# Second layer of a two-layer trunk step: the order of raw weight loads, of the attention's last splits, and of one split in the feed-forward slots

## The chip, the cores and the metric

The kernel runs on one core of one Trainium2 chip. A core has TensorE (PE, matmuls), VectorE (DVE), ScalarE (ACT), GpSimd (POOL) and SyncE (SP); each works through its own instructions in order, and they wait for each other by semaphores. SP here only issues transfers (DMA) between the chip's memory (HBM) and the on-chip memory; its queue is in order too, so a transfer that waits for its buffer holds back all that stand behind it. Matmul results go to PSUM. The metric is the device time of one execution in microseconds; the figure for the kernel is the median of three runs.

## The reference

The trunk has two layers over 128 prompt tokens and 512 sample tokens. Layer 0 mixes tokens by latent attention and pooling, layer 1 by neighbourhood attention (8 heads) and windowed attention (8 heads). Both end in a convolutional feed-forward network. The change lies in layer 1 alone:

```python
for l in range(DEPTH):
    hp = modulate(rmsnorm(xp, norm_mix[l]), mp[:, 0], mp[:, 1])
    hs = modulate(rmsnorm(xs, norm_mix[l]), ms[:, 0], ms[:, 1])
    ...
        op, kv_na, kv_sw = odd_context(hp, w_in_odd[e], swa_sink[e], w_out_odd[e])
        os_ = odd_latent(hs, cache_na_kv[:, e], cache_swa_kv[:, e], w_in_odd[e], na_rpb[e],
                         swa_sink[e], w_out_odd[e])
    ...
    xp = xp + mp[:, 2] * op
    xs = xs + ms[:, 2] * os_
    hp = modulate(rmsnorm(xp, norm_ffn[l]), mp[:, 3], mp[:, 4])
    hs = modulate(rmsnorm(xs, norm_ffn[l]), ms[:, 3], ms[:, 4])
    xp = xp + mp[:, 5] * conv_ffn(hp, w_up[l], conv_w[l], conv_b[l], w_down[l])
    xs = xs + ms[:, 5] * conv_ffn(hs, w_up[l], conv_w[l], conv_b[l], w_down[l])
```

The last matmul of both attentions is `concat(o_na, o_sw) @ w_out`, 1024 by 1024; `conv_ffn` is `(silu(g) * a) @ w_down` with `a` and `g` from a three-tap convolution of `h @ w_up`.

## The kernel before

Activations lie transposed: 8 tiles of 128 features by 642 columns (512 sample tokens, a gap, 128 prompt tokens). They are worked in two halves of columns, `EVEN`, 322 and 320 wide. The first half's parts are called `ha`, the second's `hb`.

**Products in three.** Every float32 operand is split into a high and a low part in the matmul's own format: ACT casts the high part (`split`, line 117), then another engine subtracts it from the source to get the low part (`low`, line 113, on DVE or POOL). A product then takes three matmuls for each pair of tiles: high by high, high by low, low by high. A first half of the output projection for one tile of 128 outputs is 8 x 3 = 24 matmuls of 322 columns.

**End of the attention.** `odd` works through 16 heads, two at a time in each other's shadow; the order of the steps is written out by hand as strings. `ODD_END` (line 84) is the string for the last head: `t` turns probabilities (PE transposes into `tr`, ACT copies to `pt`), `l` is the low part of `pt` on DVE, `w` weighs values (PE, into `o`), `o` and `po` add up outputs, `fo` fetches a raw tile of `w_out` for the two early products, `fs` splits it (tiles `whi`, `wlo`), and `pa` splits the attention output of one more finished pair of heads (`put_act`, line 730, into the tuples `oT`). There are 8 pairs; six `pa` steps stand in the string, and the rest is split behind it, first half and then second half.

**Early products.** `run` computes the first half of output tiles 0 and 1 (`early`) while the pool of the weights, `weights`, is still open; it reads `oT[0]` in the order 4, 5, 6, 7, 0, 1, 2, 3, which is the order in which the pairs were finished.

**Output projection.** Then `weights` is closed, a new pool `ffn1` (`pm`) opens in the same memory, and `begin` (line 1665) runs. A pool lays its tiles out in the order in which their names first appear. In `begin` these were `ht` (the sums for the feed-forward products), `x` (the residual stream), `raw` (loaded weights, three buffers). A tile's first writer waits for whatever lay there and is still in use. The first half runs over j = 0..7 (0 and 1 are the early ones): `parts(j, engine)` splits the raw weight of tile j into `w`, `add_x` adds the product to `x` on DVE (line 1605), `square` squares it on ACT. The second half runs over 3, 4, 5, 6, 7, 1, 2, 0.

**Feed-forward.** `w_up` times the normed activations is done by a scheme with 7 block products in place of 8: blocks A11, A12, A22, S1 to S4 are sums of weight blocks, p1 to p7 the products, U2 and U3 sums of products that DVE adds up (`plus`, line 1965). `slot` (line 2028) is one of the 22 tiles of the hidden width from f = 4 on, 18 of them: while PE does p1, p6, p7, p5, p2, p4, p3 of tile f, POOL makes the sums for tile f + 1 (lines 1901 to 1906), ACT and DVE or POOL split its blocks, and DVE does the additions. p3 adds into the bank of p5, so it comes after the addition (`c22`) that reads p5's result. Between p3 and the next p1 come products with `w_down`. The first slot also convolves tile 3 (`conv`).

The order on each engine is the order of the code (`manual_schedule`).

Of the kernel before, what the change touches and what calls it, by code (L numbers as in the profile page):

```python
# [81 lines left out]
jf pe m.3 e.3 n.0.a l.3 l.4 je.d w.2 pn r.2 w.3 w.4 n.1.d n.2.d r.3 n.3.d je.d o  # L82
"""]
ODD_END = """
fo.0 fo.1 t.0 pt l.0 pa t.1 fs.0 pa pl pw pa l.1 po w.0 t.2 fs.1 pa w.1 t.3 l.2 t.4 pa l.3 je w.2 w.3 pa l.4 w.4 o
"""
JOBS = ("q", 5), ("v", 1), ("q", 6), ("v", 2), ("q", 7), ("k", 0), ("q", 0), ("k", 1), ("q", 1), ("k", 2), ("q", 2), ("k", 3), ("q", 3), ("v", 3)

# [1 line left out]
class Trunk:  # L90
# [873 lines left out]
    def odd(self, pool, h, oT, bias_full, psums):  # L964
# [389 lines left out]
        def issue(plan, at, u, v):  # L1354
            nonlocal bias_next, put
            for step in plan.split():
                name, *arg = step.split(".")
                engine = arg.pop() if arg and arg[-1].isalpha() else "p"
                eng = nc.vector if engine == "d" else nc.gpsimd
                n = int(arg[0]) if arg else 0  # L1360
                if name == "j":
                    for _ in range(n):
                        job_step(at)
                elif name == "jf":
                    while job_step(at):
                        pass
                elif name == "jr":
                    job_weights(eng)
                elif name == "je":
                    job_part(at, eng)  # L1370
                elif name == "br" and at < 15:
                    bias_next = bias_of(at - 7)
                elif name == "bs" and at < 15:
                    bias_sum(*bias_next)
                elif name == "pa" and not jobs and job is None and put < (at - 1) // 2:
                    self.put_act(oT, (put + 4) % 8, o32[put], eng, EVEN)
                    put += 1
                elif name == "s" and u:
                    scores(u, n)
                elif name == "m" and u:  # L1380
                    maxima(u, n)
                elif name == "e" and u:
                    exps(u, n)
                elif name == "r" and u:
                    over(u.s, slice(n, n + 1))
                elif name == "n" and u:
                    normed(u, n, engine)
                elif name == "t" and v:
                    turn(v, n)
                elif name == "l" and v:  # L1390
                    v.t[n][3]()
                elif name == "w" and v:
                    weigh(v, n)
                elif name == "o" and v:
                    outputs(v)
                elif name == "sp" and u:
                    prompt_scores(u)
                elif name == "sv" and u:
                    prompt_take(u)
                elif name == "pe" and u and u.last:  # L1400
                    prompt_exps(u)
                elif name == "pn" and u and u.last:
                    prompt_normed(u)
                elif name == "pt" and v and v.last:
                    prompt_turn(v)
                elif name == "pl" and v and v.last:
                    v.pt[2]()
                elif name == "pw" and v and v.last:
                    prompt_weigh(v)
                elif name == "fo":  # L1410
                    self.w_first.append(self.fetch(i["w_out"][1, n], D))
                elif name == "fs":
                    self.w_first[n] = self.w_first[n](nc.gpsimd)
                elif name == "po" and v and v.last:
                    prompt_outputs(v)

        o32, v, bias_next, put, self.w_first = [], None, None, 0, []
        with self.psums(psums[1]), self.tc.manual_schedule(engines=ENGINES):
            job_load()
            with self.pool("odd_masks") as pa:  # L1420
# [20 lines left out]
                    v = u  # L1441
                issue(ODD_END, 16, None, v)
                for half in range(2):
                    for n in range(put, 8):
                        self.put_act(oT, (n + 4) % 8, o32[n], halves=EVEN, only=(half,))


# [94 lines left out]
class Mix:  # L1542
# [122 lines left out]
    def begin(self, po, oT, xsrc, early):  # L1665
# [4 lines left out]
        def load_x(j):  # L1670
            self.x[j] = self.T(self.pm, "x", [P, 2 * HB], F32, 8)
            nc.sync.dma_start(self.x[j][:, 0:W], xsrc[:, j, :])
            G.memset(self.x[j][:, W : 2 * HB], 0.0)

        def load(j, with_x=True):
            raw[j] = self.T(self.pm, "raw", [P, D], F32, 3)
            nc.sync.dma_start(raw[j], t.i["w_out"][l, j])
            if with_x:
                load_x(j)
# [6 lines left out]
        def product(j, half):  # L1686
            return self.out_product(w[j], oT, half)

        first = [self.pair(po, "first", 4) for _ in n_]
        second = [self.pair(po, "second", 4) for _ in n_]  # L1690
        rr = [self.T(po, "rs", [P, HB], F32, 3) for _ in range(3)]
        tile = lambda: self.T(po, "sq", [P, HB], F32, 3)
        ht = [[self.T(self.pm, "ht", [P, 3, HB], F32R, 8) for _ in range(2)] for _ in n_]
        load_x(0), load_x(1)
        for j in range(2, 5):
            load(j)
        parts(2, V), load(5), parts(3, G), load(6)
        sqs, sqs1 = [], []
        for j in range(KT):
# [328 lines left out]
    def slot(self, f, pv, nx, downs):  # L2028
# [11 lines left out]
        def sums(part):  # L2040
            if nx is not None:
                self.sums(nx, part)
# [7 lines left out]
        self.copy1(f)  # L2050
        conv("silu")
        self.p6(f)
        self.u2(f), sums(1), conv("aid"), block("S2")
        self.p7(f)
        self.u3(f), conv("tapa", "mul"), block("S3")
        for d in downs[:1]:
            self.parts_d(*d)
        for d in downs[2:3]:
# [267 lines left out]
```

## Time and profile before

| | |
|---|---|
| median of 3 runs (1704.79 to 1714.16) | 1706.52 us |
| profiled execution | 1716.46 us, its span 1714.7 us |
| mean granted clock of PE | 0.971 |
| busy in the span: PE, DVE, ACT, POOL | 1588.6, 1266.2, 929.1, 776.2 us |
| attention of layer 1 ends, early products begin | 1170.09 us |
| first product behind the early ones begins | 1188.42 us |
| first slot's wait of PE | 6.49 us, to 1324.83 |

In a row of the timeline stand the start, the length of a run of equal instructions, engine, line, operation, tiles, shape and count; in brackets how long the engine had been idle before it and what ended that. In a row of stretches stand the busy time of each engine with its instructions, the clock granted to PE (1.00 is full), the share of DMA in use and GB/s. In a row of groups stand the count, busy us, the mean ns of one and the engine's idle time before them. Matmuls overlap, so a run's length is a little more than the distance to the next.

### The profile page before, as it was taken

What the parts mean: (1) busy time and instruction counts of PE and PEld (TensorE: products, weight loads), DVE (VectorE), ACT (ScalarE), POOL (GpSimd) and SP (SyncE); (2) the same over time, 40 slices, a digit from 0 to 9 for tenths busy, and PEclk for the clock granted to TensorE, in tenths of its full rate; (3) what the DMA queues carried; (4) which work ended last, traced back from release to release, by engine and by line L of the source; (5) the groups of instructions that cost most, each with busy time, mean ns of one, the idle gap of its engine ahead of it and who ended that gap; (6) DMA issues with size and microseconds to landing.
All of it is one profiled execution on the core that took longest, in us unless ns stands there. A gap on an engine that the chain in (4) does not pass through costs nothing.

```text
span 1714.7 us, 28130 instructions
## 1 busy us (share of the span) xinstructions
PE 1588.6 (93%) x10349; PEld 1514.9 (88%) x10349; DVE 1266.2 (74%) x2183; ACT 929.1 (54%) x1792; POOL 776.2 (45%) x711
## 2 busy tenths in 40 slices
PE   8877888888999999999998999987997999999996
PEld 2777777788999999999997999986997999999996
DVE  4886788768899778977638777774687667777766
ACT  3554767645655335533445677874465344444435
POOL 2154677554234333433063244655235455555443
PEclk9998999989999999999999999998999999999999
DMA  9431212053344444544235211114222223222221
GB/s 339 136 105 49 62 51 80 13 174 124 117 148 145 153 139 143 155 152 136 68 107 169 59 50 53 50 39 138 86 84 75 78 73 98 82 77 73 78 73 63
DMA packets 79032, 175.62 MB, mean 102 GB/s; under 512 B 11598, under 2 KB 29342, under 8 KB 78894
## 3 DMA queue, kind: packets, MB, share of 16 engines
q1 hardware_dynamic: 76398, 169.55, 30.8%
q10 hardware_dynamic: 2304, 4.20, 0.7%
q8 instruction: 82, 1.34, 0.3%
q14 instruction: 56, 0.46, 0.1%
q0 software_dynamic: 192, 0.07, 0.0%
HBM read 166.71 MB, written 8.03 MB: 102 GB/s over the span
## 4 chain that ended last, share of the span: by engine, by line
PE 54%; DVE 12%; issue 6%; ACT 4%; POOL 3%; DMA 3%; SPq 0%; DVEq 0%; POOLq 0%; ACTq 0%
PE mm L137 26%; PE p L1594 22%; DMA mraw<-in_w_mod_dram 2%; DVE acc L316 1%; PE sc L1209 1%; DVE wlo L113 1%; PE tr L1247 1%; PE o L1259 1%; DVE nt L424 1%; DMA raw<-in_w_out_dram 1%; POOL w L113 1%; DVE ha L438 1%; ACT whi L117 1%; PE sc L137 0%; PE o L851 0%
## 5 line engine op out<-in xcount | busy, mean ns | idle before, releaser
L314 POOL TENSOR_TENSOR acc<-acc,mt 128x512 f32<-128x512 f32 x115 | 175.9, 1530 | 266.3 <-ACT mt L313 251.5
L137 PE MATMUL mm<-ha,whi 128*128 128x352 f32 (+1 forms) x1168 | 288.7, 329 | 4.7 <-ACT ha L437 4.6
L137 PE MATMUL mm<-hb,whi 128*128 128x290 f32 (+1 forms) x1168 | 244.9, 303 | 1.1 <-ACT hb L437 1.1
L137 PEld LDWEIGHTS mm<-ha,whi 128*128 128x128 f32 (+1 forms) x1168 | 203.3, 191 | 6.6 <-ACT ha L437 4.7
L316 DVE SCALAR_TENSOR_TENSOR acc<-mraw,cs,acc 128x512 f32<-128x512 f32 (+1 forms) x165 | 170.5, 1040 | 48.0 <-DMA mraw<-in_w_mod_dram 46.4
L137 PEld LDWEIGHTS mm<-hb,whi 128*128 128x128 f32 (+1 forms) x1168 | 193.6, 192 | 3.9 <-issue 2.7
L137 PE MATMUL mm<-ha,wlo 128*128 128x352 f32 (+1 forms) x584 | 189.5, 325 | 0.0
L113 POOL TENSOR_TENSOR wlo<-raw,whi 128x1024 fp32r<-128x1024 f32 (+3 forms) x47 | 100.5, 2143 | 175.1 <-ACT whi L117 107.2
L137 PE MATMUL mm<-hb,wlo 128*128 128x290 f32 (+1 forms) x584 | 175.2, 300 | 0.0
L113 POOL TENSOR_TENSOR w<-raw,w 128x512 fp32r<-128x512 f32 (+1 forms) x68 | 89.5, 1327 | 177.0 <-ACT w L117 177.0
L137 PE MATMUL mm<-g,whi 128*128 128x352 f32 (+1 forms) x704 | 157.5, 311 | 6.5 <-DVE x L447 5.2
L117 ACT CAST whi<-raw 128x1024 fp32r<-128x1024 f32 (+3 forms) x117 | 115.9, 995 | 69.0 <-PE mm L137 52.7
L313 ACT ACTIVATE mt<-mraw,cs 128x512 f32<-128x512 f32 x115 | 81.8, 721 | 111.7 <-DMA mraw<-in_w_mod_dram 99.4
L1594 PE MATMUL p<-g,d 128*128 128x320 f32 (+1 forms) x912 | 140.4, 312 | 1.0 <-POOL d L113 0.9
L1594 PEld LDWEIGHTS p<-g,d 128*128 128x128 f32 x912 | 136.9, 190 | 2.5 <-POOL d L113 2.1
L1594 PE MATMUL p<-hb,w 128*128 128x322 f32 (+1 forms) x816 | 129.5, 313 | 7.8 <-DVE cg L1965 6.5
L1594 PEld LDWEIGHTS p<-hb,w 128*128 128x128 f32 x816 | 123.5, 191 | 9.0 <-DVE cg L1965 6.8
L1594 PE MATMUL p<-ha,w 128*128 128x322 f32 x768 | 123.0, 315 | 5.8 <-ACT w L117 4.0
L137 PEld LDWEIGHTS mm<-g,whi 128*128 128x128 f32 x704 | 118.3, 189 | 8.6 <-ACT ha L437 3.8
L1594 PEld LDWEIGHTS p<-ha,w 128*128 128x128 f32 x768 | 117.5, 192 | 6.8 <-ACT w L117 4.3
L137 PEld LDWEIGHTS mm<-hb,wlo 128*128 128x128 f32 (+1 forms) x584 | 112.8, 193 | 0.0
L137 PEld LDWEIGHTS mm<-ha,wlo 128*128 128x128 f32 (+1 forms) x584 | 110.4, 189 | 0.5
(332 smaller groups left out, 3773.7 us busy)
## 6 DMA issues: line engine op xcount, KB each, us to landing
raw<-in_w_up_dram SPq DMA_DIRECT2D x90, 512.0 KB, 3.6
mraw<-in_w_mod_dram SPq DMA_DIRECT2D x128, 256.0 KB, 2.9
raw<-in_w_out_dram SPq DMA_DIRECT2D x19, 512.0 KB, 4.2
raw<-in_w_in_odd_dram SPq DMA_DIRECT2D x18, 512.0 KB, 3.5
mraw<-in_w_mod_dram SPq DMA_DIRECT2D x16, 512.0 KB, 8.8
raw<-in_w_down_dram SPq DMA_DIRECT2D x16, 512.0 KB, 3.6
draw<-in_w_down_dram SPq DMA_DIRECT2D x40, 192.0 KB, 2.4
raw<-in_w_down_dram SPq DMA_DIRECT2D x16, 384.0 KB, 3.1
```

The lines of the kernel that those rows point to most:

```text
L113: (engine or self.nc.vector).tensor_sub(lo, src, Fv(hi))
L117: self.nc.scalar.copy(hi, src)
L137: self.pe = self.nc.tensor.matmul(out, lhsT=l, rhs=r, start=k == 0, stop=k == n - 1)
L313: nc.scalar.activation(t, raw, AF.Copy, scale=s)
L314: nc.gpsimd.tensor_add(acc, acc, t)
L316: nc.vector.scalar_tensor_tensor(out=acc, in0=raw, scalar=s, in1=acc, op0=ALU.mult, op1=ALU.add)
L424: self.nc.vector.scalar_tensor_tensor(out=t[:, c], in0=x[k][:, c0:c1][:, c], scalar=self.mod[l][:, ma, k, v : v + 1], in1=rs[:, c], op0=AL ...
L438: nc.vector.scalar_tensor_tensor(out=lo[:, c], in0=t[:, c], scalar=ss, in1=Fv(hi[:, c]), op0=ALU.add, op1=ALU.subtract)
L1209: nc.tensor.matmul(ps[:, c : c + n], lhsT=u.Q[:, a], rhs=x[e], start=e == 0, stop=e == 1)
L1247: nc.tensor.transpose(tp[:, j * P : (j + 1) * P], u.p[b][:, x : x + P], self.ident)
L1259: nc.tensor.matmul(u.o[:, u.t[c][2]], lhsT=v, rhs=u.t[c][e], start=c == 0 and e == 0, stop=c == 4 and e == 1)
L1594: self.t.pe = self.nc.tensor.matmul(ps[:, 0:n], lhsT=l_, rhs=r[:, 0:n], start=first and m == 0, stop=last and m == count - 1, skip_group_c ...
```

## The change

Four edits in the code of layer 1. In `ODD_END` the second early weight's low part goes to DVE (`fs.1.d`), and `fs` takes the engine from the string. `pa` splits the first half of an attention output alone; the second halves of all eight follow behind the first halves of the last two. In `begin` the raw tiles of output tiles 2, 3 and 4 are made and loaded first, ahead of `ht` and of `x`, so that `raw` lies at the start of the pool. In `slot` the split of block S2 of tile f + 1 stands behind the addition for U3.

```diff
-fo.0 fo.1 t.0 pt l.0 pa t.1 fs.0 pa pl pw pa l.1 po w.0 t.2 fs.1 pa w.1 t.3 l.2 t.4 pa l.3 je w.2 w.3 pa l.4 w.4 o
+fo.0 fo.1 t.0 pt l.0 pa t.1 fs.0 pa pl pw pa l.1 po w.0 t.2 fs.1.d pa w.1 t.3 l.2 t.4 pa l.3 je w.2 w.3 pa l.4 w.4 o
...
-                    self.put_act(oT, (put + 4) % 8, o32[put], eng, EVEN)
+                    self.put_act(oT, (put + 4) % 8, o32[put], eng, EVEN, (0,))
...
-                    self.w_first[n] = self.w_first[n](nc.gpsimd)
+                    self.w_first[n] = self.w_first[n](eng)
...
-                    for n in range(put, 8):
+                    for n in range(0 if half else put, 8):
...
+        for j in range(2, 5):
+            load(j, False)
         first = [self.pair(po, "first", 4) for _ in n_]
...
-        load_x(0), load_x(1)
-        for j in range(2, 5):
-            load(j)
+        for j in range(5):
+            load_x(j)
...
-        self.u2(f), sums(1), conv("aid"), block("S2")
+        self.u2(f), sums(1), conv("aid")
         self.p7(f)
-        self.u3(f), conv("tapa", "mul"), block("S3")
+        self.u3(f), block("S2"), conv("tapa", "mul"), block("S3")
```

On SP, where the output projection's loads begin, before; `x` tiles are the residual stream, `raw` tiles the weights, and in brackets stand the semaphores that a load waits for:

```order
L1024 DMA out_na_v_dram<-kvo_12901 128x128 [waits DMAHW5_49,Activation_49]
L1672 DMA x_13241<-x_mid 128x642 [waits PE_49,Pool_49]
L1672 DMA x_13244<-x_mid 128x642
L1677 DMA raw_13247<-in_w_out_dram 128x1024 [waits DMAHW0_49]
L1672 DMA x_13249<-x_mid 128x642 [waits DMAHW1_49]
L1677 DMA raw_13252<-in_w_out_dram 128x1024 [waits DMAHW2_49]
L1672 DMA x_13254<-x_mid 128x642 [waits DMAHW3_49]
```

The same place now:

```order
L1024 DMA out_na_v_dram<-kvo_12901 128x128 [waits DMAHW5_49,Activation_49]
L1677 DMA raw_13222<-in_w_out_dram 128x1024 [waits DMAHW4_49,DVE_49]
L1677 DMA raw_13224<-in_w_out_dram 128x1024 [waits DMAHW0_49,Pool_49]
L1677 DMA raw_13226<-in_w_out_dram 128x1024 [waits DMAHW3_49,Pool_49]
L1672 DMA x_13247<-x_mid 128x642 [waits DMAHW1_49,PE_49]
L1672 DMA x_13250<-x_mid 128x642 [waits DMAHW2_49,PE_49]
L1672 DMA x_13253<-x_mid 128x642
```

The first load waited for a matmul of the first early product (the last that reads `wlo`, over which `x` lay) and for POOL; now it is a weight and waits for DVE, whose instruction is the low part of the second early weight (`wlo_13074` below). The first `x` waits for PE transposes and scores of the last heads.

On DVE, at the end of the attention, before (`o_2407` is the last pair's output, `ha` and `hb` are halves of attention outputs, `w` is the weight of output tile 2):

```order
L1329 TENSOR_TENSOR o_2407_12759<-tr_13057,ot_13071 64x128
L113 TENSOR_TENSOR pt_13083<-tr_13078,pt_13082 128x384 [waits Activation_49]
L113 TENSOR_TENSOR pt_13104<-tr_13099,pt_13103 128x384 [waits DVE_49,Activation_49]
L113 TENSOR_TENSOR pt_13111<-tr_13107,pt_13110 128x256 [waits Activation_49]
L1267 TENSOR_TENSOR o_2407_12759<-o_13075,ot_13137 64x4x8x16 [waits Activation_49]
L113 TENSOR_TENSOR ha_13141<-o_2326_12390,ha_13140 128x322 [waits Activation_49]
L113 TENSOR_TENSOR ha_13145<-o_2407_12759,ha_13144 128x322 [waits Activation_49]
L113 TENSOR_TENSOR hb_13149<-o_2326_12390,hb_13148 128x320 [waits Activation_49]
L113 TENSOR_TENSOR hb_13153<-o_2407_12759,hb_13152 128x320 [waits Activation_49]
```

The same place now, up to the third of the eight second halves:

```order
L1329 TENSOR_TENSOR o_2407_12759<-tr_13049,ot_13059 64x128
L113 TENSOR_TENSOR wlo_13074<-raw_13013,whi_13073 128x1024 [waits DMAHW4_49,Activation_49]
L113 TENSOR_TENSOR pt_13071<-tr_13066,pt_13070 128x384 [waits DVE_49,PE_49]
L113 TENSOR_TENSOR pt_13088<-tr_13083,pt_13087 128x384 [waits DVE_49,Activation_49]
L113 TENSOR_TENSOR pt_13095<-tr_13091,pt_13094 128x256 [waits Activation_49]
L1267 TENSOR_TENSOR o_2407_12759<-o_13063,ot_13113 64x4x8x16 [waits Activation_49]
L113 TENSOR_TENSOR ha_13117<-o_2326_12390,ha_13116 128x322 [waits Activation_49]
L113 TENSOR_TENSOR ha_13121<-o_2407_12759,ha_13120 128x322 [waits Activation_49]
L113 TENSOR_TENSOR hb_13125<-o_1850_10200,hb_13124 128x320 [waits Activation_49]
L113 TENSOR_TENSOR hb_13129<-o_1911_10508,hb_13128 128x320 [waits Activation_49]
L113 TENSOR_TENSOR hb_13133<-o_1993_10886,hb_13132 128x320 [waits Activation_49]
```

The low part of the second early weight has come from POOL to DVE and stands ahead of three `pt` low parts; six `hb` low parts have come from POOL to DVE and stand ahead of the first `w`.

On DVE, in the first slot (f = 4), one piece of the difference; `ca_14603` is U2's sum, the `cg` with it is U3's, `w` from `s` is S2's low part:

```order
-L1965 TENSOR_TENSOR ca_14603<-p_14606,ca_14603 128x322
-L113 TENSOR_TENSOR w_2805_14626<-s_14594,w_2804_14625 128x512
-L1965 TENSOR_TENSOR cg_14642<-p_14629,ca_14603 128x322
-L1996 SCALAR_TENSOR_TENSOR v_14623<-ca_14513,convw,v_14623 128x641 x2
-L2019 TENSOR_TENSOR va_14646<-v_14623,cg_14514 128x642
+L1997 SCALAR_TENSOR_TENSOR v_14565<-cg_14514,convw,v_14565 128x641 x2
+L1966 TENSOR_TENSOR ca_14603<-p_14606,ca_14603 128x322
+L1966 TENSOR_TENSOR cg_14638<-p_14625,ca_14603 128x322
+L113 TENSOR_TENSOR w_2807_14641<-s_14594,w_2806_14640 128x512
+L1997 SCALAR_TENSOR_TENSOR v_14623<-ca_14513,convw,v_14623 128x641 x2
+L2020 TENSOR_TENSOR va_14646<-v_14623,cg_14514 128x642
```

The addition for U3 has changed places with S2's low part.

## Prediction

> **What bounds the kernel now.** I read the busy time by stretches first, then the timeline of TensorE (PE) where it is not full, then what the others did there. All times are us from the span's start.
>
> ```profile
> 1180.00:1200.00 20.00, 15.71 (x86) 15.18 (x85) 6.15 (x11) 7.05 (x14) 5.13 (x6) 0.85 0.88 292
> 1200.00:1220.00 20.00, 20.00 (x135) 19.84 (x134) 7.56 (x18) 5.33 (x10) 2.53 (x2) 1.00 0.23 77
> 1400.00:1500.00 100.00, 99.82 (x671) 99.08 (x670) 74.82 (x128) 44.02 (x78) 55.23 (x44) 1.00 0.26 81
> ```
>
> The columns are PE, its weight loads, DVE, ACT, POOL, clock, DMA share and GB/s. Behind 1200 PE is the bound: 135 matmuls in 20 us is 148 ns each, and in the slots (1400 to 1500) only 0.18 us of 100 is idle. In 1180 to 1200 it is neither full nor at full clock. This is the seam between the attention of layer 2 and its output projection:
>
> ```profile
> 1170.09 0.74 PE L1594 MATMUL p<-ha,whi 128*128 128x322 f32 x2
> ...
> 1173.16 0.41 PE L1594 MATMUL p<-ha,whi 128*128 128x322 f32 x1 [0.47 <-POOL ha L113]
> ...
> 1175.19 0.41 PE L1594 MATMUL p<-ha,whi 128*128 128x322 f32 x1 [1.33 <-POOL ha L113]
> ...
> 1176.97 0.64 PE L1594 MATMUL p<-ha,whi 128*128 128x322 f32 x1 [0.95 <-POOL ha L113]
> ...
> 1188.42 0.57 PE L1594 MATMUL p<-ha,w 128*128 128x322 f32 x2 [3.99 <-ACT w L117]
> 1189.28 23.03 PE L1594 MATMUL p<-ha,w 128*128 128x322 f32 x142 [0.30 <-DVE w L113]
> ```
>
> From 1170.09 on PE runs the two early products (2 x 24 matmuls), then the six other first halves (6 x 24, the 2 + 142 of the last rows), to 1189.28 + 23.03 = 1212.31. That is **42.2 us for 192 matmuls**, where 192 x 148 ns is 28.4. Of the 13.8 too many, 0.47 + 1.33 + 0.95 + 3.99 + 0.30 = **7.0 are waits**: three for POOL's low halves of `ha`, two for the first raw weights. The other **6.8 are half clock**:
>
> ```profile
> 1170.00:1172.00 2.00, 2.00 (x10) 0.50 0.00 0
> ...
> 1178.00:1180.00 2.00, 2.00 (x9) 0.50 0.04 8
> 1180.00:1182.00 2.00, 2.00 (x10) 0.50 0.49 138
> ...
> 1186.00:1188.00 2.00, 0.00 (x0) 1.00 0.98 360
> ...
> 1190.00:1192.00 2.00, 2.00 (x9) 0.50 1.01 317
> ...
> 1194.00:1196.00 2.00, 2.00 (x16) 1.00 0.83 323
> ```
>
> The clock column falls to 0.50 some us after a gap (1190 to 1192, behind the 3.99 us), and then 9 or 10 matmuls fit where 15 or 16 do later. The weights are late because of one queue:
>
> ```profile
> SPq L1672 <- PE p L1594: 26.4, 1, 26.4
> ...
> 1181.02 0.42 SPq L1677 DMA_DIRECT2D raw<-in_w_out_dram  x1
> ...
> 1187.23 1.14 ACT L117 CAST w<-raw 128x512 fp32r<-128x512 f32 x2 [14.33 <-DMA raw<-in_w_out_dram]
> ```
>
> SP stood 26.4 us before the first `x` load, until a PE matmul of the first early product freed the memory under `x` (1179.5). The first raw load behind it was issued at 1181.02 and its cast could start at 1187.23, 6.2 us later.
>
> **The change, part by part.** *Raw first.* In the program of the change the first raw load waits for DVE's low half of `wlo` for the second early weight alone, and the `x` loads wait for PE work that was over before 1160. So the end of that low half sets the first load.
>
> *Low half on DVE, second halves later.* These rows set its time and the attention's end:
>
> ```profile
> 1165.62 0.37 ACT L1327 COPY ot<-tr 64x256 f32<-64x256 f32 x1
> ...
> 1166.38 1.05 ACT L117 CAST whi<-raw 128x1024 fp32r<-128x1024 f32 x1
> ...
> 1166.63 0.56 DVE L113 TENSOR_TENSOR pt<-tr,pt 128x384 fp32r<-128x384 f32 x1
> ```
>
> And these are the lengths of one instruction, from the groups by line and form (min/median/max, or busy us and mean ns):
>
> ```profile
> L113 DVE TENSOR_TENSOR wlo<-raw,whi x70: 1181/1224/2312, 287.8 to 1118.8; 128x1024 fp32r<-128x1024 f32 x70
> ...
> L113 DVE TENSOR_TENSOR ha<-o,ha 128x322 fp32r<-128x322 f32 x2 | 1.7, 910 | 0.0
> L113 DVE TENSOR_TENSOR hb<-o,hb 128x320 fp32r<-128x320 f32 x2 | 2.1, 1093 | 0.0
> ...
> L113 DVE TENSOR_TENSOR hb<-second,hb x8: 486/495/496, 1255.9 to 1264.8; 128x322 fp32r<-128x322 f32 x8
> ...
> L113 POOL TENSOR_TENSOR ha<-o,ha 128x322 fp32r<-128x322 f32 x6 | 5.7, 950 | 2.2 <-ACT ha L117 2.2
> L117 ACT CAST hb<-o 128x320 fp32r<-128x320 f32 x8 | 3.6, 463 | 0.0
> ```
>
> Two casts of `hb` leave ACT ahead of the copy at 1165.62 (they start 0.36 apart), so `whi` is cast at 1165.7 and done at 1166.7. DVE's low half of it takes 1.2 (median) to 2.3 (maximum). It runs beside POOL's lows, and beside those the `ha` lows took 0.910 against 0.495 for the same shape elsewhere, so I take 1.22 x 0.910 / 0.495 = 2.2: done at 1168.9. Behind it in DVE's queue stands the `pt` low that began at 1166.63; it now ends at 1169.5 instead of 1167.2. PE, the last two transposes and the last `o` matmuls wait for it. Before, 2.9 us lay between that low and 1170.09, with casts of `whi`, `ha` and `hb` ahead of ACT's copy; without these I estimate 1.9 from the lengths of the four steps (about 0.4 each for transposes, copy and low, 0.7 for matmuls). The early products start at **1171.3, 1.2 later** (bounds 1170.4 with a low of 1.2, and 1172.5 with 2.3 and 2.9).
>
> They then wait for nothing. POOL has one 2.4 us `wlo` and six `ha` lows of 0.95 in a row, no longer six `hb` lows between, and is through by about 1172.2. The last two `ha` lows are DVE's, done by 1174; at full clock the eighth `ha` is asked for 21 matmuls behind the start, 1174.4. So **2.75 us of waits go**. Of the clock I keep one cold stretch as long as that of 1190 (3.4 us, of which 148 against 268 ns loses 1.5; bounds 0 and 3). The early products end at 1171.3 + 48 x 0.148 + 1.5 = **1179.9**.
>
> Is the third weight there by then? Its load is issued at 1168.9 and, with the 6.2 us of before, lands at 1175.1. ACT casts `ha` until 1173.3, then eight `hb` in 3.6 us, then `w` in 1.1: 1178.0. DVE ends its `ha` lows at 1174, then has eight `hb` lows (six of them new), 4.0 us at 0.495 with POOL idle: 1178.0, and the first `w` low 0.7 later, 1178.7. That is 1.2 us ahead of need, so **4.3 us of waits go** and nothing is late next; the cover is these 1.2 us. No gap, no cold stretch: 144 x 0.148 = 21.3, end at 1201.2 instead of 1212.31: **11.1 us earlier** (7.0 of waits + 5.3 of clock - 1.2). The `x` loads and the `x` memsets of POOL move with the queue; each `x` is asked for at the end of its product, later than the weight, and costs nothing. Behind 1201 PE was full and loads waited for buffers, so I carry the whole shift to the end.
>
> By the Trainium skill, TensorE: Matmul & The Clock Gate, "What's actually happening", the array goes to half clock after an idle window of about 3.4 us and back after a busy one, on windows that run freely. By that rule the cold stretch behind the gap goes with the gap; were it there for another reason, the sum would be 1.5 us less. The row agrees as far as 1190 to 1192 at 0.50 behind 3.99 us of idleness goes.
>
> *S2 behind U3.* Only the first slot (f = 4) has PE waiting for this chain:
>
> ```profile
> 1316.64 0.49 DVE L1965 TENSOR_TENSOR ca<-p,ca 128x322 f32<-128x322 f32 x1
> 1319.50 1.20 DVE L113 TENSOR_TENSOR w<-s,w 128x512 fp32r<-128x512 f32 x1 [2.38 <-ACT w L117]
> 1320.63 0.48 DVE L1965 TENSOR_TENSOR cg<-p,ca 128x322 f32<-128x322 f32 x1
> ...
> 1324.30 0.48 DVE L1965 TENSOR_TENSOR cg<-p,cg 128x322 f32<-128x322 f32 x1
> ...
> 1324.83 3.59 PE L1594 MATMUL p<-hb,w 128*128 128x322 f32 x12 [6.49 <-DVE cg L1965]
> ```
>
> PE waits 6.49 for the addition at 1324.30. The addition for U3 (1320.63) moves into the 2.38 us in which DVE waited for S2's cast, so the chain gets shorter by it alone: **0.4 us** (bounds 0 and 0.5). S2's cast still waits for POOL's difference, and its low half still starts at 1319.50 on this clock. In the other slots nothing waits:
>
> ```profile
> 1448.95 0.49 DVE L1965 TENSOR_TENSOR cg<-p,cg 128x322 f32<-128x322 f32 x1
> ...
> 1452.31 1.93 PE L1594 MATMUL p<-hb,w 128*128 128x322 f32 x12
> ```
>
> The addition to which PE comes back is done 2.9 us early there; a swap of two neighbours on DVE moves it by less than 1: nothing.
>
> Sum: -11.1 - 0.4 = **-11.5 us**. The profiled execution took 1716.46 (span 1714.7), so 1705.0 for it; the median of the three runs is 1706.52, 9.9 below that, and with the same gain comes to **1695.0**. About 0.5%, 8.5 us, is what a measurement of this kernel can tell from no change.
>
> **The rivals.** *The shift is eaten behind 1212.* DVE, ACT and POOL convert weights up to 1325, and the 6.49 us wait could belong to their own backlog and not follow PE. Then what is left by 1325 is about half, 5 to 6 us: 1701. Against it: the casts and loads wait for buffers that PE frees. *DVE becomes the bound.* If the eight `hb` lows take 1.09, as the two beside POOL did, they end at 1174 + 8.7 = 1182.7 and PE waits 3.5 for the first `w` low: gain 8.0, 1698.5. By the Trainium skill, SBUF — State Buffer, "Who interferes with whom", DVE with two SBUF inputs and a reading GpSimd shut each other out, and not once POOL is done; by that rule this rival falls away and 1695.0 stands. The 1.09 and 0.495 agree with it. *The load is not early*: the chain ACT, `wlo`, SP slips by as much as it gained, say because the DVE low sits behind a late copy; the waits for weights stay and only 2.75 of waits go, less 1.2: 1705. *Slower, by the swap*: S2's low now stands behind an addition that waits for PE, and all DVE work of 17 slots stands behind it. It decides from a delay of 2.9 us in a slot on. At 4.2 us each slot would lose 1.3, and 17 x 1.3 - 11.1 is 11 slower, 1717.5. Against it, S2's low has the whole of a slot until it is needed, and U3's wait ends with a product of 1.8 us.
>
> **How the numbers follow.** Forecast 0.68, eaten 0.14, DVE 0.08, load not early 0.06, slower 0.04. The forecast's own bounds are the start (1170.4 to 1172.5), the cold stretch (0 to 3 us) and the runs' own spread (1704.8 to 1714.2): gains of 8 to 14.5, 1692 to 1698.5. To leave out no more than 2 in 10 the range takes in the eaten shift and some spread: 1690 to 1703. Faster by over 8.5 us: most of the forecast, part of the DVE case, 0.65; within: 0.30; slower 0.05.
>
> **What would show it.** In the profile of the changed kernel: SP's first raw load near 1169; no wait of PE over 1 us between the early products and the third; the six first halves over by about 1201; the 0.50 clock gone behind the early products; the matmuls that stood at 1324.83 near 1313, their wait about 6 us. It is wrong if the third product waits for `w`, if the early products start behind 1173, or if the wait in the first slot grows by what was gained.

## The result and the profile after

The changed kernel takes 1700.3 us (median of 10 runs, 1698.38 to 1703.3), the kernel before 1711.42 us (median of 10 runs beside them, 1704.79 to 1715.78): ratio **0.9934**, 95% interval 0.9925 to 0.9943; the medians lie 11.1 us apart. The profiled execution has a span of 1701.5 us against 1714.7.

Not all of those 13.2 us belong to the change. Traces are compared here from one common point ahead of it, the three transposes of the last head that wait for `p`, to the first matmul of `hb` (the end of the first halves): the *seam*. In the timeline of PE, before:

```profile
1160.15 0.55 PE L1247 MATMUL tr<-ident,p 128*128 128x128 f32 x3 [0.43 <-DVE p L1235]
...
1212.15 3.71 PE L1594 MATMUL p<-hb,w 128*128 128x320 f32 x24
```

and in the changed kernel:

```profile
1157.63 0.55 PE L1247 MATMUL tr<-ident,p 128*128 128x128 f32 x3 [0.44 <-DVE p L1235]
...
1166.51 0.69 PE L1247 MATMUL tr<-ident,p 128*128 128x128 f32 x2 [2.13 <-DVE pt L113]
...
1168.70 0.74 PE L1594 MATMUL p<-ha,whi 128*128 128x322 f32 x2
...
1177.29 21.73 PE L1594 MATMUL p<-ha,w 128*128 128x322 f32 x144
1198.86 3.67 PE L1594 MATMUL p<-hb,w 128*128 128x320 f32 x24
```

The point lies 2.52 us earlier in work that the change doesn't touch; the seam went from 52.00 to 41.23, **10.77 shorter**. The last row but one is a single run of 144 matmuls with no wait ahead of it: the third weight and the weights behind it are in time. The stretches show the clock (columns: PE, its weight loads, DVE, ACT, POOL, clock, DMA share, GB/s):

```profile
1180.00:1200.00 20.00, 20.00 (x135) 20.00 (x135) 7.39 (x15) 5.82 (x12) 5.08 (x4) 1.00 0.48 161
...
1158.00:1160.00 2.00, 0.88 (x7) 0.54 (x5) 1.59 (x3) 1.22 (x3) 0.49 (x1) 0.55 0.00 0
...
1168.00:1170.00 2.00, 2.00 (x9) 2.00 (x8) 0.45 (x2) 1.28 (x3) 1.91 (x8) 0.50 1.02 408
1170.00:1172.00 2.00, 2.00 (x9) 2.00 (x9) 1.96 (x5) 1.67 (x5) 0.00 (x0) 0.54 0.99 383
1172.00:1174.00 2.00, 2.00 (x16) 2.00 (x15) 2.00 (x6) 2.00 (x6) 0.00 (x0) 1.00 1.05 410
```

1180 to 1200 is full at 1.00, where it had 15.71 us of work at 0.85. One half-clock stretch is left. It begins in the attention, between 1158 and 1160, lies under the first early matmuls too, and ends by 1172. On SP the weights now go first, 15.0 us sooner than at 1181.02, 12.5 of it from the common point:

```profile
1166.01 1.28 SPq L1677 DMA_DIRECT2D raw<-in_w_out_dram  x3
1167.38 2.41 SPq L1672 DMA_DIRECT2D x<-x_mid  x5
```

And DVE at the same place, with the new low half ahead of `pt`, then the eight `hb` lows, then the third weight:

```profile
1164.22 1.76 DVE L113 TENSOR_TENSOR wlo<-raw,whi 128x1024 fp32r<-128x1024 f32 x1 [0.87 <-ACT whi L117]
1165.91 1.01 DVE L113 TENSOR_TENSOR pt<-tr,pt 128x384 fp32r<-128x384 f32 x2
...
1171.24 3.30 DVE L113 TENSOR_TENSOR hb<-o,hb 128x320 fp32r<-128x320 f32 x8
1174.45 1.29 DVE L113 TENSOR_TENSOR w<-raw,w 128x512 fp32r<-128x512 f32 x2
```

The first of the two `w` lows is done at about 1175.1 and PE asks for it at 1177.29: 2.2 us of cover.

### The profile page after: what moved, and what is told of

Its sections match the earlier page's. It is cut to its first block, busy times and chain, and to the rows that moved or that the text cites. A ratio compares the mean times of both kernels' runs of the same rounds, so it can differ in the third digit from the quotient of the medians.

```text
span 1701.5 us, 28135 instructions
## 1 busy us (share of the span) xinstructions
PE 1584.5 (93%) x10349; PEld 1512.7 (89%) x10349; DVE 1260.4 (74%) x2190; ACT 929.0 (55%) x1792; POOL 770.5 (45%) x704
## 4 chain that ended last, share of the span: by engine, by line
PE 49%; DVE 16%; issue 6%; ACT 5%; DMA 5%; POOL 1%; SPq 0%; DVEq 0%; ACTq 0%; POOLq 0%
PE p L1594 24%; PE mm L137 19%; DMA mraw<-in_w_mod_dram 4%; DVE wlo L113 2%; DVE acc L316 2%; PE sc L1209 1%; PE tr L1247 1%; PE o L1259 1%; DVE u L511 1%; DVE nt L424 1%; ACT whi L117 1%; DVE ha L438 1%; DVE g L113 1%; DVE v L1997 1%; ACT mt L313 1%
```

## The experiments

All are read in the same way: the seam, and from its end to the last matmuls that sum squares (they start at 1702.14 before, at 1688.70 after). Us, worked out from those rows of each trace; the ratio is to the kernel before.

| kernel | seam | seam's end to last | both | ratio, 95% interval |
|---|---|---|---|---|
| before | 52.00 | 489.99 | 541.99 | 1 |
| changed | 41.23 | 489.84 | 531.07 | 0.9934, 0.9925 to 0.9943 |
| e1 x first | 47.86 | 491.24 | 539.10 | 0.9989, 0.9980 to 0.9998 |
| e2 S2 ahead | 41.19 | 490.07 | 531.26 | 0.9950, 0.9932 to 0.9968 |
| e3 `wlo` on POOL | 41.73 | 491.56 | 533.29 | 0.9931, 0.9916 to 0.9946 |
| e4 both halves | 41.56 | 491.44 | 533.00 | 0.9939, 0.9922 to 0.9957 |
| e5 raw first only | 45.43 | 492.40 | 537.83 | 0.9970, 0.9959 to 0.9981 |
| e6 first slot | 40.92 | 489.27 | 530.19 | 0.9934, 0.9919 to 0.9950 |
| e7 low later | 38.45 | 489.93 | 528.38 | 0.9924, 0.9907 to 0.9941 |
| e8 both moves | 38.43 | 488.74 | 527.17 | 0.9914, 0.9897 to 0.9932 |
| e9 convolution ahead | 38.45 | 488.52 | 526.97 | 0.9923, 0.9905 to 0.9940 |
| e10 taps first | 38.72 | 489.82 | 528.54 | 0.9935, 0.9917 to 0.9954 |
| e11 changed again | 41.48 | 489.68 | 531.16 | 0.9950, 0.9935 to 0.9966 |
| e12 S3 behind c22 | 41.14 | 492.69 | 533.83 | one run |

**e1: the order of the pool undone.**

```diff
-        for j in range(2, 5):
-            load(j, False)
...
-        for j in range(5):
-            load_x(j)
+        load_x(0), load_x(1)
+        for j in range(2, 5):
+            load(j)
```

> The changed kernel with one part undone: in `begin` the loads of `x` lie first in the pool again, ahead of those of the raw weights; the `ha` lows, the DVE low of `wlo` and the place of S2 stay as changed. My theory (the order of the pool is what brought the third weight early): SP's first raw load waits again for the end of an early product, some 6 us before its weight can be cast, so that it is issued near the first early product's end and not at 1166. PE then waits some 3.5 to 5 us for the cast or the low half of the third weight, and 1 to 1.5 us more go in matmuls of 268 ns at half clock behind that wait. That is 5 to 6 us slower than the changed kernel: ratio to the kernel before 0.9965 to 0.997. Rival (the order is immaterial, since the casts and lows of `hb` stand ahead of the weight on ACT and DVE anyway): the third product waits for less than 1 us and the ratio stays at 0.993 to 0.994.

SP's queue, and PE, in e1:

```profile
1173.62 1.84 SPq L1672 DMA_DIRECT2D x<-x_mid  x2
1175.51 0.43 SPq L1677 DMA_DIRECT2D raw<-in_w_out_dram  x1
```

```profile
1181.73 24.34 PE L1594 MATMUL p<-ha,w 128*128 128x322 f32 x144 [4.92 <-ACT w L117]
1205.91 3.67 PE L1594 MATMUL p<-hb,w 128*128 128x320 f32 x24
```

The wait is back as expected, 4.92 us, and behind it the 144 matmuls take 24.34 and not 21.73: 2.6 lost to half clock, not 1 to 1.5. The seam is 6.6 longer than in the changed kernel and 1.4 more is lost later, so 1.9 us is left of the gain and not 5 or 6. The mechanism holds, and its price was too low: 0.9989 lies outside the expected 0.9965 to 0.997.

**e2: S2 ahead of U3 again.**

```diff
-        self.u2(f), sums(1), conv("aid")
+        self.u2(f), sums(1), conv("aid"), block("S2")
...
-        self.u3(f), block("S2"), conv("tapa", "mul"), block("S3")
+        self.u3(f), conv("tapa", "mul"), block("S3")
```

> The changed kernel with S2's split back ahead of p7 and U3, all else as changed. The prediction's term (the swap shortens the chain in the first slot by 0.4 us): from ACT's copy of L1960 in the first slot to the addition of c22 it takes 10.6 to 10.9 us and not 10.43, PE's wait for that addition is near 7.0 and not 6.66, and the ratio to the kernel before is 0.0002 to 0.0003 higher, which the time alone cannot tell. The rival, from the trace of the changed kernel (the addition of c22 stands behind the `d` low on DVE, whose cast on ACT waits for POOL, so that the place of U3's addition decides nothing): that distance stays at 10.2 to 10.5, the wait at 6.3 to 6.7, and the ratio within 0.001 of 0.9934. If the swap costs in the other slots, the ratio falls below 0.9925.

In e2 it takes 10.53 us from ACT's copy (line 1960, 1301.94) to c22's addition (1312.47), against 10.43 in the changed kernel, and PE waits 6.77 against 6.66: 0.1, not 0.4. The ratio is 0.0016 above that of the changed kernel, more than the rival allowed, but e11, the changed kernel once more, gave 0.9950 too. What took the 0.4 is seen on POOL and DVE. POOL before, then DVE before; `s` is the first sum of the slot, the `w` low that of S3:

```profile
1316.17 1.29 POOL L1901 TENSOR_TENSOR s<-raw 128x512 f32<-128x512 f32 x1
...
1322.56 1.26 POOL L113 TENSOR_TENSOR w<-raw,w 128x512 fp32r<-128x512 f32 x1 [0.73 <-ACT w L117]
```

```profile
1323.61 0.77 DVE L113 TENSOR_TENSOR d<-draw,d 128x512 fp32r<-128x512 f32 x1
1324.30 0.48 DVE L1965 TENSOR_TENSOR cg<-p,cg 128x322 f32<-128x322 f32 x1
```

The same two places in the changed kernel:

```profile
1303.54 1.30 POOL L1902 TENSOR_TENSOR s<-raw 128x512 f32<-128x512 f32 x1 [0.20 <-DMA raw<-in_w_up_dram]
...
1309.94 1.27 POOL L113 TENSOR_TENSOR w<-raw,w 128x512 fp32r<-128x512 f32 x1 [0.73 <-ACT w L117]
```

```profile
1304.42 0.49 DVE L1966 TENSOR_TENSOR cg<-p,ca 128x322 f32<-128x322 f32 x1
...
1310.60 1.17 DVE L113 TENSOR_TENSOR d<-draw,d 128x512 fp32r<-128x512 f32 x1
1311.68 0.48 DVE L1966 TENSOR_TENSOR cg<-p,cg 128x322 f32<-128x322 f32 x1
```

and PE there:

```profile
1312.22 3.38 PE L1594 MATMUL p<-hb,w 128*128 128x322 f32 x12 [6.66 <-DVE cg L1966]
```

U3's addition is out of the way at 1304.42, and the `d` low does begin 0.4 earlier against POOL's sums (7.06 behind the first, 7.44 before). But now more of it lies beside POOL's low, which ends at 1311.21, and it takes 1.17 and not 0.77. c22 begins 8.13 us behind POOL's first sum before, 8.14 after, 8.13 in e2 and in e11. What PE's wait moved by, 6.49 before and 6.66 after, comes from ahead of that sum: it waits 0.20 for a weight load now. The Trainium skill, SBUF — State Buffer, "Who interferes with whom", has a DVE instruction with two SBUF inputs contend with a reading GpSimd instruction for a shared port, and the second one wait; by that rule the 0.4 was lost from the start, and the two lengths of the `d` low agree with it.

**e3: `wlo` on POOL again.**

```diff
-fo.0 fo.1 ... po w.0 t.2 fs.1.d pa w.1 ...
+fo.0 fo.1 ... po w.0 t.2 fs.1 pa w.1 ...
```

> The changed kernel with the low half of the second early weight (`wlo`) on POOL again and not on DVE. My theory (the DVE low costs the early products 1.1 us at their start, by standing ahead of the `pt` low, and gives nothing but cover): the early products start about 1 us earlier against the last `pt` cast than 10.48, POOL's `ha` lows come 2.4 us later, so that one or two early products wait for up to 1 us, the first raw load is issued 1 to 3 us later, and the third product waits for 0 to 1 us since its weight had 2.2 us of cover. Net within 1 us of the changed kernel: ratio to the kernel before 0.993 to 0.9945. Rival (the low on DVE is what frees POOL in time): waits for POOL's lows of 2 us and more return and the third weight comes late, with a ratio of 0.996 or more.

PE in e3:

```profile
1166.29 0.46 PE L1594 MATMUL p<-ha,whi 128*128 128x322 f32 x2
...
1169.38 0.41 PE L1594 MATMUL p<-ha,whi 128*128 128x322 f32 x1 [1.44 <-POOL ha L113]
...
1170.47 0.41 PE L1594 MATMUL p<-ha,whi 128*128 128x322 f32 x1 [0.38 <-POOL ha L113]
...
1171.55 0.41 PE L1594 MATMUL p<-ha,whi 128*128 128x322 f32 x1 [0.38 <-POOL ha L113]
```

The early products start 8.50 behind the common point and not 11.07: 2.6 earlier. They then wait 2.2 us for POOL, and the third weight is in time. The net is 0.5 at the seam, and the time can't be told from the changed kernel's: as the theory had it, with both of its parts larger.

**e4: `pa` splits both halves.**

```diff
-                    self.put_act(oT, (put + 4) % 8, o32[put], eng, EVEN, (0,))
+                    self.put_act(oT, (put + 4) % 8, o32[put], eng, EVEN)
...
-                    for n in range(0 if half else put, 8):
+                    for n in range(put, 8):
```

> The changed kernel with `pa` splitting both halves of an attention output again; the raw weights lie first, `wlo` stays on DVE, S2 behind U3. My theory (two thirds of the gain hang on the weights, a third on POOL's `ha` lows; and the halves matter to both, since a POOL with `hb` lows between frees the raw and `wlo` buffers no earlier): the early products wait for POOL's `ha` lows again, 1.5 to 4 us in two or three waits, partly at 268 ns, and no wait for the third weight, since the load is issued as early as in the changed kernel. 3 to 6 us slower than the changed kernel: ratio to the kernel before 0.995 to 0.997. Rival (all the gain is the order of the pool): the early products' waits are hidden or replaced, and the ratio stays at 0.993 to 0.994.

My theory fell. No early product waits, although POOL has its `hb` lows between the `ha` lows again. The early products start 0.85 us later (11.92 behind the common point), since PE waits 1.16 and not 0.45 for DVE's `o` ahead of them, and lose less to half clock; the seam is 0.3 longer. The ratio, 0.9939, is the rival's figure, but not its reason: e5 shows that the order of the pool is not the whole gain.

**e5: the order of the pool alone**, on the kernel before.

```diff
+        for j in range(2, 5):
+            load(j, False)
...
-        load_x(0), load_x(1)
-        for j in range(2, 5):
-            load(j)
+        for j in range(5):
+            load_x(j)
```

> The kernel before with one part of the change alone: the raw weights lie first in the pool of `begin`. `wlo` stays on POOL, `pa` splits both halves, S2 stays ahead of U3. In the two runs with one of the two POOL parts undone (the low on POOL, or both halves) the seam was only 0.5 and 0.3 us longer than in the changed kernel, so each of them does the other's work. Theory: with both undone POOL has two `wlo` lows and twelve `ha` and `hb` lows in a row again; the early products wait for `ha` lows some 2.75 us in three waits and run partly at half clock, but the first raw load goes when the second `wlo` low is done, near 1172 on the clock of before and not at 1181, and the third product waits for less than 0.5 us. From the early start to the first matmul of `hb`: 42.06 us before, about 35 here. Ratio to the kernel before 0.9955 to 0.9965. Rival A (the order of the pool is the whole gain): 0.993 to 0.9945. Rival B (the order of the pool alone brings nothing while POOL is late, as the x-first run brought little with POOL relieved): 0.998 to 1.0, with a wait for the third weight of over 2 us.

PE's waits in e5, between 1156 and 1190 (total, times, longest):

```profile
PE p L1594 <- POOL ha L113: 2.7, 3, 1.3
```

Here the three waits stand as before, the clock is at 0.50 for most of 1172 to 1178, and the third product waits for nothing. From the early start to the end of the seam it is 35.49 us for 192 matmuls: 7.1 over 28.4, of which 2.7 are waits and 4.4 clock; in the changed kernel it is 30.16, 1.8 over. So the theory holds, though the ratio lies a little above the expected 0.9955 to 0.9965, and the seam adds up: 6.57 by the pool's order alone (e5), 4.14 by everything else alone (e1), 10.77 together. Of that 4.14, the low on DVE and the late second halves each bring nearly all by themselves: added to e5's order of the pool, the first takes 3.87 off the seam (e4), the second 3.70 (e3).

**e6 and e7: two moves that the trace suggests.** e6 puts U3, p5, c22 and the `d` split ahead of S2, the convolution and S3 in the first slot; e7 moves the DVE low of `wlo` behind the last `pt` low.

```diff
-        self.u3(f), block("S2"), conv("tapa", "mul"), block("S3")
...
+        self.u3(f)
+        if pv is not None:
+            self.p5(f)
+            self.c22(f)
+            for d in downs[:1]:
+                self.parts_d(*d)
+        block("S2"), conv("tapa", "mul"), block("S3")
...
```

```diff
-... po w.0 t.2 fs.1.d pa w.1 t.3 l.2 t.4 pa l.3 je w.2 w.3 pa l.4 w.4 o
+... po w.0 t.2 pa w.1 t.3 l.2 t.4 pa l.3 je w.2 w.3 pa l.4 fs.1.d w.4 o
```

> The changed kernel with one order in one slot: in the first slot of the second layer's feed-forward (f = 4) the products and additions of U3, p5 and c22 stand ahead of S2's split, the products `tapa` and `mul` and S3's split, and no longer behind them; the other 17 slots stay. Theory: PE's wait of 6.66 us for c22's addition is the queue of DVE and POOL (the lows of `w` and `d` ahead of it), not the data, so it falls to 0 to 2 us; S2's and S3's weights come later and take back 1 to 3 us of that. 3 to 6 us faster than the changed kernel: ratio to the kernel before 0.990 to 0.9915. Rival (the chain is bound by POOL's sums and the weights of the next product, which then wait in its place): within 1 us of the changed kernel, 0.993 to 0.994, with the wait moved to the next product of weights.

> The changed kernel with the DVE low of `wlo` moved behind the last `pt` low of the attention (it stands ahead of three of them now). Theory (the 1.1 us by which the early products start later come from the low standing ahead of the `pt` low, and nothing needs `wlo` that early, since the second early product begins 24 matmuls behind the first): PE's wait of 2.1 us for `pt` falls below 0.5, the early products start 1.5 to 2.5 us earlier, up to 1 us of that goes in waits for the `ha` lows, the first raw load is issued 1 to 2 us later and its 2.2 us of cover falls to 0 to 1. 0.5 to 2 us faster than the changed kernel: ratio to the kernel before 0.992 to 0.9935. Rival (the `ha` lows or the third weight take its place): the first matmul of `hb` starts within 0.3 us of where it starts in the changed kernel, measured from the same cast of `pt`.

PE in e6:

```profile
1302.70 2.05 PE L1594 MATMUL p<-hb,w 128*128 128x322 f32 x12
1304.59 1.87 PE L1594 MATMUL p<-g,d 128*128 128x322 f32 x9
1310.20 0.64 PE L1594 MATMUL p<-g,d 128*128 128x322 f32 x1 [3.73 <-ACT g L2024]
```

The 6.66 us wait for c22's addition is gone: the 12 matmuls that waited start at 1302.70. A wait of 3.73 stands in the next product, which needs tile 3's convolved `g`; that waited on DVE behind S2's low (1.76 us). The half clock stays, and the time is the changed kernel's (0.9 less by the trace): the rival. In e7:

```profile
1164.40 1.30 PE L1247 MATMUL tr<-ident,p 128*128 128x128 f32 x5 [0.45 <-DVE o L1329]
...
1166.99 0.46 PE L1594 MATMUL p<-ha,whi 128*128 128x322 f32 x2
...
1170.19 0.42 PE L1594 MATMUL p<-ha,whi 128*128 128x322 f32 x1 [0.64 <-POOL ha L113]
```

The wait of 2.13 for `pt` is gone (all five transposes in one run), the early products start 2.6 earlier, soon at full clock, and 0.64 is given back. The seam is 2.8 shorter, more than expected; the ratio, 0.9924, lies in what was expected.

**e8, e9, e10: the two together, and two orders of the first slot on top.** e9 puts S2's split behind `tapa` and `mul`; e10 puts these ahead of the `d` split too.

```diff
-        block("S2"), conv("tapa", "mul"), block("S3")
+        conv("tapa", "mul"), block("S2", "S3")
```

```diff
+            conv("tapa", "mul")
             for d in downs[:1]:
                 self.parts_d(*d)
+            conv("ghi", "glo")
...
-        block("S2"), conv("tapa", "mul"), block("S3")
+        block("S2", "S3")
...
```

> The changed kernel with the two moves together: the DVE low of `wlo` behind the last `pt` low, and U3, p5 and c22 ahead of S2 and S3 in the first slot. Theory: they lie 100 us apart on the same chain and add up: 3.5 to 7 us faster than the changed kernel, ratio to the kernel before 0.989 to 0.991. Rival (what one gives the next wait for a weight takes): no better than the better of the two alone.

> The kernel with both moves (the low of `wlo` later; U3, p5 and c22 ahead in the first slot), and in that slot S2's split now behind `tapa` and `mul`, so that DVE has the `d` low, the two taps, the product `va`, and then S2's low. In the run with both moves PE waited 3.06 us for `g`, and in the run with the slot alone 3.73; `g` follows `va`, and ahead of the taps stood S2's low with 1.76 us. Theory (that queue is what PE waits for, not data): the wait for `g` falls by 1.5 to 1.8, to 1.3 to 2.2 us, and up to 1.5 us of half clock behind it go too. 1 to 3 us faster than with both moves: ratio to the kernel before 0.9895 to 0.991. Rival (the taps wait for their own input, ACT's `v` or POOL): the wait stays above 2.7 us and the ratio at 0.991 to 0.992.

> As the run before, but with the taps and `va` ahead of the `d` low too, and the split of `g` right behind the `d` low, ahead of S2's. The first matmuls of `g` by `d` then wait for `d`, whose low starts some 2.6 us later (two taps and `va`), and no longer the later ones for `g`. Theory: one wait of 1.5 to 2.5 us for `d` and none over 0.5 for `g`; within 1 us of the run before, ratio to the kernel before 0.9895 to 0.991. Rival (the low of `d` runs beside POOL and takes 1.75 again, and the wait for `d` grows to 3 us or more): no gain on the run with both moves, 0.991 to 0.992.

e8 keeps the 2.8 of e7 and gains 1.1 behind the seam, as the table has it; its ratio misses the expected 0.989 to 0.991 narrowly, and its interval overlaps that of e7. In e9 the wait for `g` fell from 3.06 in e8 to 2.04, by 1.0 and not by the 1.5 to 1.8 expected. The time did not follow: 0.6 of it went again in the nine matmuls ahead (1.89 against 1.50) and in the wait behind (0.45 against 0.23), and half clock still lies on the matmuls behind that (62 in 11.89, 11.83 in e8):

```profile
1309.49 0.63 PE L1594 MATMUL p<-g,d 128*128 128x322 f32 x1 [2.04 <-ACT g L2024]
1310.58 11.89 PE L1594 MATMUL p<-g,d 128*128 128x322 f32 x62 [0.45 <-DVE g L113]
```

In e10 the waits go to `d` instead (2.6 us in three for DVE, 2.5 for ACT), and the gain of the slot is lost: 0.9935, where 0.9895 to 0.991 was expected and its rival had 0.991 to 0.992. The best kernels are e8 and e9, which can't be told apart; nor can e7 from them by the time.

**e11: the changed kernel again**, measured beside e9 and e10.

> The changed kernel as it is, once more, on the same chip and against the same runs of the kernel before as the two runs ahead of it. Theory and rivals alike: ratio to the kernel before within its first interval, 0.9925 to 0.9943, and a seam of 41.23 us from the transposes that wait for `p` to the first matmul of `hb`, to 0.3. It gives the distance of the two combined kernels to the changed one, and shows how far the profile's clock of the part ahead of the seam moves from run to run.

The seam repeats to 0.25; the ratio, 0.9950, is 0.0016 higher than the first and out of what I expected. Beside it e9 took 1700.41 (1699.18 to 1700.81, 4 runs) against 1704.73 (1703.84 to 1706.05, 5 runs): 4.3 less, with no overlap. e9 beats both kernels.

**e12: S3 behind c22** in the first slot.

```diff
-        self.u3(f), block("S2"), conv("tapa", "mul"), block("S3")
+        self.u3(f), block("S2"), conv("tapa", "mul")
+        if pv is None:
+            block("S3")
...
+        if pv is not None:
+            block("S3")
```

> The changed kernel with S3's split, in the first slot alone, behind c22's addition and no longer ahead of the `d` low. In four runs so far (the kernel before, the changed one twice, and the one with S2 ahead) POOL's first sum of the first slot begins 8.13 to 8.14 us ahead of c22's addition, whatever the place of S2, and c22 begins 0.47 to 0.48 us behind the end of POOL's low of S3. Theory: the `d` low on DVE cannot end while that POOL low runs, and this is where the 0.4 us went that the swap saved; without the POOL low beside it the `d` low takes 0.69 to 0.77 us and not 1.17, c22 begins 7.7 to 7.8 us behind the first sum, and PE's wait is 6.2 to 6.3 us. Rival (POOL's sums or ACT's cast of `d` set it, and the 8.13 is theirs): it stays at 8.1 to 8.2, with a wait of 6.5 to 6.7. One look, so the time tells nothing here.

It didn't separate the two: only ACT's cast moved behind that of `d`, and POOL's low, which follows the cast and not c22, still lay beside the `d` low (first POOL, then DVE):

```profile
1313.63 1.27 POOL L113 TENSOR_TENSOR w<-raw,w 128x512 fp32r<-128x512 f32 x1 [0.73 <-ACT w L117]
```

```profile
1314.28 1.17 DVE L113 TENSOR_TENSOR d<-draw,d 128x512 fp32r<-128x512 f32 x1
1315.37 0.48 DVE L1966 TENSOR_TENSOR cg<-p,cg 128x322 f32<-128x322 f32 x1
```

`d` was cast 2.5 us earlier here (1310.44, S3's raw at 1312.93), and c22 still came 8.15 behind the first sum (1307.22) and 0.47 behind the end of POOL's low. So the time of ACT's cast of `d` is not what sets it. That POOL's low is, fits all nine traces in which the `d` low stands between it and c22 (before, changed, e1 to e5, e11, e12: c22 0.46 to 0.48 behind the end of that low), but no run took that low away. e6 took c22 out from behind the `d` low: it then begins 1.6 us behind POOL's first sum (1302.15 and 1300.54), so the 8.1 us are the queue's and not the data's.

The pair of e6 and e8 shows the hold in another place. In e6 the `d` low begins 0.08 us behind POOL's third sum:

```profile
1303.28 1.29 POOL L1906 TENSOR_TENSOR s<-raw,s 128x512 f32<-128x512 f32 x1
1303.36 1.75 DVE L113 TENSOR_TENSOR d<-draw,d 128x512 fp32r<-128x512 f32 x1 [0.71 <-ACT d L117]
```

and in e8 0.05 us ahead of it:

```profile
1298.95 0.69 DVE L113 TENSOR_TENSOR d<-draw,d 128x512 fp32r<-128x512 f32 x1 [0.71 <-ACT d L117]
```

There the `d` low takes 0.69, and POOL's sum, begun at 1299.00, takes 1.79 and not 1.29. In these two runs the one that begins second takes longer, DVE or POOL.

## Why the prediction was right, and where it was not

**The seam** came out by its own steps, though not each of them. On the common point's clock: early start 1.2 later, measured 1.13; no wait in the early products, none measured; 1.5 us of half clock in them, measured 8.59 us for 48 matmuls where 7.1 is full speed; early end 19.75 behind the point (1179.9), measured 19.66; the 144 in 21.3, measured 21.6; 11.1 gained, measured 10.77. e1 shows that the pool's order carries the third product's wait, e5 that it carries it alone. Two agreements are partly luck. The later start is two errors that cancel: `wlo`'s low took 1.76 and not 2.2, and from the `pt` low to the first early matmul it took 2.2 (1166.51 to 1168.70) and not 1.9. And the 1.5 us of half clock were borrowed from the stretch at 1190, while what was measured is the end of one that began in the attention, ahead of the early products; the prediction had no step for that.

**The cover of the third weight** was mis-sized: 1.2 us, measured 2.2. The eight `hb` lows were charged with 0.495 each, 4.0 in all; each is 0.48 long, but with POOL idle they start 0.40 apart and take 3.30, and ACT's eight casts 2.98 and not 3.6. In e3, where POOL still has `ha` lows, some are up to 1.16 long and the eight take 4.65. The rival of 1.09 each has its mechanism there, but not its place: POOL was done at 1169.7 in the changed kernel, ahead of the first `hb` low.

**What removes the 2.75 of waits.** The text gave them to one `wlo` and no `hb` lows on POOL, both together. The waits themselves are gone with one `wlo` alone (e4) and back at 2.2 without it (e3), 2.7 without both (e5). For the seam either is nearly enough (e3 costs 0.5, e4 0.3), since e3 starts its early products 2.6 earlier. The sum was right, and the need for both wasn't: the waits hang on the single `wlo`, and the seam on either of the two.

**S2 behind U3, -0.4,** is the step that failed. The prediction let the chain on DVE get shorter "by it alone", with the `d` low as long as before. The low grew by the same 0.4 beside POOL's (1.17 and not 0.77), c22 kept its 8.13 from POOL's first sum, and PE's wait is 6.66 and not near 6. The term is worth 0 to 0.1 us; that POOL's low is the cause fits every trace and was not isolated by a run. That nothing happens in the other 17 slots, and that the swap does not cost there, held: e2 has the same time behind the seam to 0.2.

**The whole shift to the end** held in this pair of traces: 489.99 and 489.84 from the seam's end. It is not a rule: e3 and e4, with the changed kernel's code there, and e5, with that of the kernel before, have 491.4 to 492.4. In e3 the 72 products with `w_down` that follow the first slot's wait take 12.02, in the changed kernel 10.91; more of them fall into half clock (0.74 granted in 1300 to 1320, 0.83 there in the changed kernel). In e1, 1.4 longer behind the seam, they take 10.88; where its loss lies was not taken apart. The rival of an eaten shift needed 5 to 6 us, and is out.

**The time itself,** 1695.0, is 5.3 below the measured 1700.3, with the gain right to 0.4 (11.5 against 11.1 between the medians). That is closer than the gain repeats: e11 has 8.9 between its medians. The term that was off is the base: 1706.52, the median of three runs, where ten gave 1711.42 and the later measurements 1711 to 1714. The profiled execution itself, 1716.46, lay above; leaning on three runs was the choice that cost 5.

## What to carry to other kernels

Where the first load of a new stage stands late in a queue, look at which old tile its memory lay under, and lay the tile that is asked for first over what is done with first: it was worth 6.6 of the seam by itself. Before taking an addition or a low half off a chain, find the other engine's work that ends beside it, and measure the distance to that work's start; if it stays the same, as the 8.13 us did, taking something off the chain gains nothing; putting the awaited step ahead of the instruction that is held up does, as e6 did with c22 (though the next wait took most of it). And a new instruction belongs behind what PE waits for next, not where its input is ready: moving the `wlo` low behind three `pt` lows gave 2.8 us more.

## What the runs showed of the hardware that was not expected

Half clock came without a long gap. In e3 PE ran at 1.00 from 1166 on, had three waits of 1.44, 0.38 and 0.38, and then fell to 0.50 (columns as before):

```profile
1168.00:1170.00 2.00, 0.62 (x3) 0.45 (x3) 2.00 (x3) 2.00 (x6) 2.00 (x3) 1.00 0.38 55
1170.00:1172.00 2.00, 1.24 (x7) 0.90 (x7) 2.00 (x3) 1.26 (x5) 1.69 (x8) 0.99 0.95 379
1172.00:1174.00 2.00, 2.00 (x9) 2.00 (x8) 2.00 (x6) 1.86 (x4) 0.06 (x1) 0.50 1.02 399
```

PE was busy 1.86 us of 4 there. The Trainium skill, TensorE: Matmul & The Clock Gate, "What's actually happening", asks for an idle window of about 3.4 us; here the longest gap was 1.44, and the measurement decides. It fell with PE busier too: in the changed kernel the clock stood at 1.00 from 1154 to 1158 with PE busy 2.89 us of 4 and no gap over 0.45, and was 0.55 in the two us behind. What counts as idle is not shown here. And taking a wait from 3.06 to 2.04, as e9 did against e8, did not bring the clock back.

The part ahead of the seam, the same in all these kernels, ends (at the common point) between 1153.13 (e8) and 1161.26 (e12) on the traces' clocks. These 8 us are as much as most of the differences studied here; spans are to be compared only from a common point, and where this scatter comes from was not taken apart.
